# The norms of a decoder layer: nine events placed in a list, a smaller held part, and the embedding's product inside the norm

## The chip, the cores and the metric

One core of a Trainium2 chip runs the whole layer in one launch. The metric is device time in microseconds (us), median of the runs shown. The engines are named as in the profile: PE multiplies matrices (PEld is its loading of weights), DVE and ACT are the vector and the scalar engine, POOL does a little, SP issues nearly all transfers (SPq). Each engine executes its own instructions in the order in which the program lists them.

## The reference, cut to what matters

256 tokens of width 2048 pass through a layer with four layer norms. `alpha` is 2 to the power 1/4.

```python
def layer_norm(x, g, b):
    mu = jnp.mean(xf, axis=-1, keepdims=True)
    var = jnp.mean(jnp.square(xf - mu), axis=-1, keepdims=True)
    y = (xf - mu) * lax.rsqrt(var + LN_EPS)
    return (y * g.astype(jnp.float32) + b.astype(jnp.float32)).astype(x.dtype)
...
h = layer_norm(alpha * h + 0.5 * swiglu(h, w_ffn1_gu[i], w_ffn1_down[i]), ln_g[i, 0], ln_b[i, 0])
...
mixed = (jax.nn.sigmoid(gate_r) * ret_branch + jax.nn.sigmoid(gate_a) * att_branch) @ w_mix_out[i]
h = layer_norm(alpha * h + mixed, ln_g[i, 1], ln_b[i, 1])
h = layer_norm(alpha * h + 0.5 * swiglu(h, w_ffn2_gu[i], w_ffn2_down[i]), ln_g[i, 2], ln_b[i, 2])
ple = jax.nn.sigmoid(h @ w_ple_gate[i]) * (p[i] @ w_ple_proj[i])
h = layer_norm(alpha * h + ple, ln_g[i, 3], ln_b[i, 3])
```

The first three norms are the ones that the change touches. They are called here the first norm (after the first feed-forward part, tiles f1y), the second (after the mixers, mixy) and the third (after the second feed-forward part, f2y). `p @ w_ple_proj` depends on no norm; the kernel computes it early and puts it by.

## The kernel before, in words

**Products and chunks.** Every float32 product is made of three: each operand is split into a high and a low part, and `Sum.add` (L291 to L293) issues low x high, high x high, high x low, each 128x128 by 128x512. Weights come in chunks of 512 KB. A chunk is loaded by SP (L105) into one slot, and then made (`split`, L91 and L92): ACT casts it into a slot of high parts, DVE subtracts into a slot of low parts, and the raw slot is free again. The 256 tokens are two tiles, t = 0 and t = 1. One chunk serves two depths kk of 128, so it is 2 x 3 matmuls for each t, 12 for both.

**Slots.** All chunks and most other tiles live in 46 slots of 4 KB per partition. `fill` (L184 on) lists loads and makes ahead of the products: `room["slots"]` is the number of slots that chunks may take, `room["ahead"]` how much work of PE shall be made beforehand (a plain chunk counts 12), `room["far"]` the same for loads; no make is listed while `room["quiet"]` is set. A slot is taken again only after its last reader is done.

**A norm.** It must not stop PE, so it is spread over both token tiles. `held_out` (from L399) runs the last chunks of the product before the norm ("held" chunks) for t = 0 only, keeps them, then runs them for t = 1. These are called the first and the second pass. After the first pass `Norm.normal(0)` is listed: DVE adds the last columns (`columns`), takes the statistics, computes 1/sqrt in nine small steps (`rsqrt`) and normalises the first 512 columns in two halves (L478, L479). Within the second pass, `turn(0, c)` for c = 0 to 3 normalises 512 further columns on DVE (`more`, one group ahead, listed before the rest of the turn), lets PE transpose group c (`ln_turn`, L486, four transposes), ACT cast and DVE subtract it into the next product's left operand (`ht`, L91 and L92). `run` is given the counts at which the four turns stand: a count is three matmuls (one kk of one chunk, t = 1). After the second pass `normal(1)` is listed.

Then the next product starts in `Norm.first`: six chunks for t = 0, kept, then the same six for t = 1; `turn(1, c)` stands at given counts of chunks. `quiet` is set in the last two steps of the first pass and taken back at the last turn of `first`.

**What differs between the three.** The first norm holds 3 pairs x 2 columns = 6 chunks (f1_down) and `first` belongs to the first block of the mixers (w_rv). The second holds 5 chunks of w_mix (`HELD_MIX`), and `first` belongs to the first block of the second feed-forward part. The third holds 6 chunks (f2_down), and `first` belongs to the gate of the embedding (w_pg). After the first and the second norm's second pass, `put_by` computes two blocks of `p @ w_ple_proj` (four matmul groups of six, tiles pp), copies them by ACT and stores them; it stands between the second pass and `first`.

Of the kernel before, what the change touches and what calls it, by code (L numbers as in the profile page):

```python
# [15 lines left out]
P = 128  # L16
# [10 lines left out]
KF = FF // P  # L27


HELD_MIX = 5  # L30
FRONT = 6
FRONT_PAIRS = 3
HELD_PAIRS = 3
SLOTS = 46


# [12 lines left out]
def layer(ctx: ExitStack, tc: tile.TileContext, io):  # L49
# [163 lines left out]
    def done(u):  # L213
        room["used"] -= u.keeps
        fill()
# [4 lines left out]
    def quiet(on):  # L220
        room["quiet"] = on
# [272 lines left out]
    class Norm:  # L494
# [32 lines left out]
            else:  # L527
                ln_turn(*args, 4 * c, 4, self.keep.get(c))

        def run(self, steps, lhs, turns):  # L530


            self.vectors = vectors.pop()
            self.new = big.tile([P, KD, 512], F32R, tag="ht", name=f"ht{self.i}")
            per = len(steps) // len(self.cols)

            def of_columns(t, j):
                if (j + 1) % per == 0 and j + 1 < len(steps):
                    self.columns(t, j // per)

            def between(n):
                for c, when in enumerate(turns):
                    if n == when:
                        self.turn(0, c)

            held_out(steps, lhs, self.sums, of_columns, lambda: self.normal(0), between)
            self.normal(1)

        def put_away(self):
            if self.away is not None:  # L550
                for c in range(4):
                    sync.dma_start(self.away[c], self.y[c])

        def first(self, steps, lhs, sums, turns):

            def hook(n):
                for c, when in enumerate(turns):
                    if n == when:  # L560
                        self.turn(1, c)

            kept = []
            for j, (key, k0, n) in enumerate(steps):
                u = take(key)
                kept.append(u)
                tokens_chunk(u.chunk, k0, lhs, [sums[t][n] for t in range(2)], (0,))
                fill()
                hook(j + 1)
                if j + 1 == max(turns):  # L570
                    quiet(False)
            for j, (key, k0, n) in enumerate(steps):
                tokens_chunk(kept[j].chunk, k0, lhs, [sums[t][n] for t in range(2)], (1,))
                done(kept[j])
                hook(len(steps) + j + 1)
                if len(steps) + j + 1 == max(turns):
                    quiet(False)
            quiet(False)
            self.put_away()

    def block_stats(stats, y, col):
# [21 lines left out]
            split(pt[:, :, :S], pt[:, :, S:], raw)  # L603
            p_parts.append(pt)

    def put_by(blks):

        pt = p_parts.pop()
        lhs = lambda k: (pt[:, k, :S], pt[:, k, S:])
        done_blks = []  # L610
        for blk in blks:
            u = take(("w_pp", blk, 0))
            ps = banks(f"pp{blk}")
            tokens_chunk(u.chunk, 0, lhs, [Sum(b, 2) for b in ps], (0, 1))
            done(u)
            done_blks.append((blk, ps))
        for blk, ps in done_blks:
            v = slot([P, 2, 512], F32, f"pps{blk}")
            for t in range(2):
                act.copy(v[:, t], ps[t])  # L620
            pp[blk] = dram.tile([P, 2, 512], F32, name=f"ppd{blk}")
            sync.dma_start(pp[blk], v)
# [69 lines left out]
    def gu_keys(name, j):  # L692
        return lambda n, p: (name + "_gu", j, n, p)

    def down_units():
# [11 lines left out]
        return first, second + [("P", p) for p in rest[:-HELD_PAIRS]], rest[-HELD_PAIRS:]  # L707

    def down_keys(name, b):
        return lambda n, p: (name + "_down", 2 * b + n, p)  # L710
# [1 line left out]
    def plan_ffn(name):  # L712
        for j in range(KF // 4):
            block_units(gu_units(j), gu_keys(name, j))
        first, second, held = down_units()
        block_units(first, down_keys(name, 0))
        block_units(second, down_keys(name, 1))
        plan.extend(Single(down_keys(name, 1)(n, p)) for n in range(2) for p in held)

    def ffn(name, i, ht, norm, keep, residual, keepers, away):  # L720
# [28 lines left out]
        for j in range(KF // 4):  # L749
            pg, pu = banks(f"{name}g{j}"), banks(f"{name}u{j}")  # L750
            units = gu_units(j)
            plain = len(units) - sum(kind == "S" for kind, p in units)
            n_of = {(0, 0): KD, (0, 1): KD, (1, 0): KD, (1, 1): KD}
            for kind, p in units:
                if kind == "S":
                    for at in ((0, 0), (0, 1), (1, 0)):
                        n_of[at] -= 1
                    n_of[1, 1] -= 2
            sums = [[Sum((pg, pu)[n][t], n_of[t, n]) for n in range(2)] for t in range(2)]
            got = []  # L760

            if norm is not None and j == 0:
                front, units = units[:FRONT_PAIRS], units[FRONT_PAIRS:]
                steps = [(gu_keys(name, 0)(n, p), 2 * p, n) for _, p in front for n in range(2)]
                norm.first(steps, rhs, sums, (2, 3, 4, 6))
                slots_for_weights(24)

            def before(u, j=j, offset=KD // 2 - len(units)):
                u += offset
                if j == 0 and norm is None and u % 2 == 0:  # L770
                    first_chunk(u // 2)
                    if u == 6:
# [12 lines left out]
            if got:  # L785
                g, v = got
                for x, ps in ((g, pg), (v, pu)):
                    for t in range(2):
                        dve.tensor_tensor(x[:, t], x[:, t], ps[t], ALU.add)  # L789
                act.activation(g, g, AF.Silu)  # L790
                dve.tensor_tensor(v, g, v, ALU.mult)
            else:
                v = slot([P, 2, 512], F32, f"{name}v{j}")
                for t in range(2):
                    act.activation(v[:, t], pg[t], AF.Silu)
                for t in range(2):
                    dve.tensor_tensor(v[:, t], v[:, t], pu[t], ALU.mult)
            later(2, lambda j=j, v=v: turned(j, v))
# [10 lines left out]
        first, second, held = down_units()  # L809
        n_of = {}  # L810
        for b, units in enumerate((first, second + [("P", p) for p in held])):
            s = sum(kind == "S" for kind, p in units)
# [28 lines left out]
            block_stats(stats, y, n)  # L841


        last_ahead = 160 if i < 2 else 136
        last = {}
        for at, (kind, p) in enumerate(second + [("P", p) for p in held]):
            last[p // 2] = at
# [10 lines left out]
        pt_ = [banks(f"{name}e{t}") for t in range(2)]  # L858
        sums = [[Sum(pt_[t][n], n_of[1][t, n]) for n in range(2)] for t in range(2)]
        block(f"{name}d1", second, down_keys(name, 1), lhs, forms, sums, fold(1), before_unit)  # L860
        slots_for_weights(30, last_ahead, last_ahead + 24)
        steps = [(down_keys(name, 1)(n, p), 2 * p, n) for n in range(2) for p in held]

        def combine(sl, p):
            dve.tensor_tensor(sl, sl, p, ALU.add)

        norm = Norm((2, 3), sums, combine, y, stats, i, 4 * LN_EPS, keepers, away)
        norm.run(steps, lhs, (8, 9, 11, 12))
        return norm


# [45 lines left out]
    def mixers(ht, norm, residual, keepers, away):  # L917
# [17 lines left out]

        ps = banks("rv0")
        sums = [[Sum(ps[t], KD)] for t in range(2)]
        norm.first([(("w_rv", 0, c), 2 * c, 0) for c in range(FRONT)], rhs, sums, (2, 3, 4, 6))
        slots_for_weights(24)
        for c in range(FRONT, KD // 2):  # L940
            u = take(("w_rv", 0, c))
# [287 lines left out]
        sums = [[Sum(ps[t], KD)] for t in range(2)]  # L1229
        make_for_norm()  # L1230
        first = KD // 2 - HELD_MIX
        slots_for_weights(28, 148, 172)
        for c in range(first):
            u = take(("w_mix", 3, c))
            tokens_chunk(u.chunk, 2 * c, lhs, [sums[t][0] for t in range(2)], (0, 1))
# [1 line left out]
            run_side()  # L1237
        steps = [(("w_mix", 3, c), 2 * c, 0) for c in range(first, KD // 2)]
        norm = Norm((3,), sums, combine, y, stats, 1, LN_EPS, keepers, away)
        norm.run(steps, lhs, (8, 9, 10, 10))  # L1240
        return norm


    def embedding(ht, norm, y):
# [17 lines left out]
        for blk in range(4):  # L1262
# [4 lines left out]
            if blk == 0:  # L1267
                for j in range(4):
                    pp[j] = load_columns(pp, j, "ppr")
                steps = [(key + (c,), 2 * c, 0) for c in range(FRONT)]  # L1270
                norm.first(steps, lhs, [[s] for s in sums], (4, 5, 6, 8))
                slots_for_weights(24)
                for c in range(FRONT, KD // 2):
                    u = take(key + (c,))
# [53 lines left out]
    with tc.manual_schedule():  # L1328
# [118 lines left out]
```

## Time and profile before

| | us |
|---|---|
| median of 3 runs (2318.96 to 2320.65) | 2319.98 |
| profiled execution | 2320.46 |
| its span, first to last instruction | 2318.6 |
| PE busy in the span | 2281.9 (98%) |
| DVE busy | 1871.6 (81%) |
| ACT busy | 1163.8 (50%) |
| idle time of PE ahead of the transposes of the three norms | 9.9, 3.1 and 2.6 |

The time of the execution is 1.9 us more than the span. A row of the timeline gives the start, the duration, the engine, the line, the operation, the tiles (written <- read) and in brackets the idle time ahead of it with what ended it. The view by windows gives for each stretch the busy time of each engine with its count of instructions, then the granted TensorE clock (1.00 is full), the busy share of the transfer engines and GB/s.

### The profile page before, as it was taken

The numbers are of one execution on the slowest core, as the hardware profiler recorded it, in microseconds if no ns is written. First come the engines' busy times: TensorE is split into PE (matmuls) and PEld (weight loads), VectorE is DVE, ScalarE is ACT, GpSimd is POOL, SyncE is SP. The second block draws the span as 40 slices with busy tenths as digits, with TensorE's granted clock in tenths as the row PEclk, the third lists the DMA queues.
The fourth block names the chain that finished last, engine by engine and source line by source line (L and its number), as shares of the span: only waits on it lengthen the run. The fifth ranks groups of instructions, "written<-read, shape, count | busy, mean of one in ns | idle before, by whom it ended". The sixth has DMA issues, their size and how long they took to land.

```text
span 2318.6 us, 28626 instructions
## 1 busy us (share of the span) xinstructions
PE 2281.9 (98%) x10502; PEld 1889.0 (81%) x10502; DVE 1871.6 (81%) x2348; ACT 1163.8 (50%) x1404; POOL 96.9 (4%) x53
## 2 busy tenths in 40 slices
PE   9999999999998999999999999999999999999997
PEld 7788888888886888888777888788888888888876
DVE  7999999988987774677555555779999999889876
ACT  5565555565553342434544534345555565555532
POOL 0000000000000430133000000000000000000000
PEclk9999999999998999999999999999999999999999
DMA  9566666665585565546556657476666566565771
GB/s 315 164 217 192 195 209 195 193 215 190 197 290 225 193 216 166 172 146 200 156 162 182 190 187 274 161 253 188 196 198 205 179 199 218 190 217 191 273 271 55
DMA packets 193724, 465.69 MB, mean 201 GB/s; under 512 B 14768, under 2 KB 16048, under 8 KB 193584
## 3 DMA queue, kind: packets, MB, share of 16 engines
q1 hardware_dynamic: 191456, 460.91, 60.4%
q10 hardware_dynamic: 2128, 2.97, 0.4%
q8 instruction: 82, 1.34, 0.2%
q14 instruction: 58, 0.48, 0.1%
HBM read 455.43 MB, written 8.39 MB: 200 GB/s over the span
## 4 chain that ended last, share of the span: by engine, by line
PE 94%; DVE 4%; DMA 1%; issue 1%; ACT 0%; SPq 0%; DVEq 0%; ACTq 0%
PE f2g L291 3%; PE f2g L293 3%; PE f2g L292 3%; PE gt L291 3%; PE f1g L291 3%; PE f1g L292 3%; PE f1g L293 3%; PE rqk L242 3%; PE gt L292 3%; PE gt L293 3%; PE f2u L291 2%; PE f2u L292 2%; PE f2u L293 2%; PE f1u L291 2%; PE f1u L292 2%; PE f1u L293 2%
## 5 line engine op out<-in xcount | busy, mean ns | idle before, releaser
L92 DVE TENSOR_TENSOR lf_gu<-rf_gu,hf_gu 128x1024 fp32r<-128x1024 f32 (+1 forms) x283 | 334.5, 1215 | 10.5 <-ACT hf_gu L91 10.1
L91 ACT CAST hf_gu<-rf_gu 128x1024 fp32r<-128x1024 f32 (+1 forms) x283 | 282.1, 1046 | 22.3 <-DMA rf_gu<-in_f_gu 21.4
L92 DVE TENSOR_TENSOR lw_in_f<-rw_in_f,hw_in_f 128x1024 fp32r<-128x1024 f32 x148 | 208.1, 1439 | 61.7 <-ACT hw_in_f L91 59.1
L92 DVE TENSOR_TENSOR lf_down<-rf_down,hf_down 128x1024 fp32r<-128x1024 f32 x152 | 181.1, 1220 | 29.8 <-ACT hf_down L91 24.7
L91 ACT CAST hf_down<-rf_down 128x1024 fp32r<-128x1024 f32 x152 | 155.6, 1051 | 80.3 <-DMA rf_down<-in_f_down 26.4
L91 ACT CAST huf_gu<-uf_gu 128x1024 fp32r<-128x1024 f32 x70 | 73.8, 1054 | 159.2 <-DVE uf_gu L164 153.4
L91 ACT CAST hw_in_f<-rw_in_f 128x1024 fp32r<-128x1024 f32 x148 | 145.9, 1052 | 0.2
L291 PE MATMUL gt<-hw_in_f,ht 128*128 128x512 f32 x256 | 102.5, 400 | 0.0
L291 PE MATMUL f1g<-hf_gu,xt 128*128 128x512 f32 x247 | 97.2, 394 | 5.3 <-ACT hf_gu L91 5.3
L292 PE MATMUL gt<-hw_in_f,ht 128*128 128x512 f32 x256 | 99.9, 390 | 0.0
L293 PE MATMUL gt<-lw_in_f,ht 128*128 128x512 f32 x256 | 99.9, 390 | 0.0
L293 PE MATMUL f1g<-lf_gu,xt 128*128 128x512 f32 x247 | 97.1, 393 | 0.0
L292 PE MATMUL f1g<-hf_gu,xt 128*128 128x512 f32 x247 | 97.0, 393 | 0.0
L291 PE MATMUL f2g<-hf_gu,ht 128*128 128x512 f32 x247 | 96.4, 390 | 0.0
L293 PE MATMUL f2g<-lf_gu,ht 128*128 128x512 f32 x247 | 96.2, 389 | 0.0
L292 PE MATMUL f2g<-hf_gu,ht 128*128 128x512 f32 x247 | 96.1, 389 | 0.0
L91 ACT CAST hvf_gu<-vf_gu 128x1024 fp32r<-128x1024 f32 x70 | 73.8, 1054 | 29.2 <-DVE vf_gu L166 29.1
L92 DVE TENSOR_TENSOR luf_gu<-uf_gu,huf_gu 128x1024 fp32r<-128x1024 f32 x70 | 85.3, 1218 | 0.0
L92 DVE TENSOR_TENSOR lvf_gu<-vf_gu,hvf_gu 128x1024 fp32r<-128x1024 f32 x70 | 85.3, 1218 | 0.0
L790 ACT ACTIVATE eve<-eve 128x1024 f32<-128x1024 f32 x20 | 21.2, 1062 | 126.7 <-DVE eve L789 126.7
L291 PE MATMUL f1u<-hf_gu,xt 128*128 128x512 f32 x212 | 83.6, 394 | 0.0
L291 PE MATMUL f2u<-hf_gu,ht 128*128 128x512 f32 x212 | 83.5, 394 | 0.0
(1053 smaller groups left out, 6278.8 us busy)
## 6 DMA issues: line engine op xcount, KB each, us to landing
rf_gu<-in_f_gu SPq DMA_DIRECT2D x351, 512.0 KB, 4.9
rf_down<-in_f_down SPq DMA_DIRECT2D x176, 512.0 KB, 4.5
rw_in_f<-in_w_in_f SPq DMA_DIRECT2D x148, 512.0 KB, 3.9
rw_rv<-in_w_rv SPq DMA_DIRECT2D x32, 512.0 KB, 4.6
rw_ret<-in_w_ret SPq DMA_DIRECT2D x32, 512.0 KB, 4.3
rw_mix<-in_w_mix SPq DMA_DIRECT2D x32, 512.0 KB, 4.7
rw_pg<-in_w_pg SPq DMA_DIRECT2D x32, 512.0 KB, 5.4
rw_att<-in_w_att SPq DMA_DIRECT2D x16, 512.0 KB, 3.9
```

Of the source, the lines that this page charges most:

```text
L91: act.copy(dst_hi, src)
L92: (lo_engine or dve).tensor_tensor(dst_lo, src, dst_hi, ALU.subtract)
L242: pe.matmul(ps[f], hi[:, kk, f * P : (f + 1) * P], rhs(k), start=k == 0, stop=k == n_k - 1,)
L291: pe.matmul(o, al, bh, start=first, stop=False)
L292: pe.matmul(o, ah, bh, start=False, stop=False)
L293: pe.matmul(o, ah, bl, start=False, stop=self.left == 0)
L790: act.activation(g, g, AF.Silu)
```

## The change

1. `run` and `first` no longer hold fixed hooks. A norm has nine events in one order: `turn(0, 0)` to `turn(0, 3)`, `normal(1)`, `turn(1, 0)` to `turn(1, 3)`; `follow` fires the next ones when a count is reached. The lists given to `run` and `first` say at which counts.
2. For the first and the second norm, `put_by` runs inside `run`, right after the second pass, and the turns of t = 0 stand among its four groups of six matmuls. Its product is now ordered by t within a chunk.
3. `HELD_MIX` is 4 (was 5); the first norm holds 2 pairs = 4 chunks (was 6), the third still 3 pairs.
4. The first and second norm want 136 ahead (160 and 148 before), the third as before; the slots for chunks while the norm runs are 27, 26 and 27 (30, 28 and 30 before).
5. `quiet` ends at the ninth event instead of the last hook of `first`.

```diff
-HELD_MIX = 5
+HELD_MIX = 4
...
-HELD_PAIRS = 3
+HELD_PAIRS = 2, 3
...
+        def follow(self, n, times):
+            while times and times[0] == n:
+                times.pop(0)
+                at, self.at = self.at, self.at + 1
+                if at == 4:
+                    self.normal(1)
+                else:
+                    self.turn(at // 5, at % 5)
+                if at == 8:
+                    quiet(False)
+
-        def run(self, steps, lhs, turns):
+        def run(self, steps, lhs, times, blks=()):
...
+            self.at, times = 0, list(times)
...
-            def between(n):
-                for c, when in enumerate(turns):
-                    if n == when:
-                        self.turn(0, c)
-
-            held_out(steps, lhs, self.sums, of_columns, lambda: self.normal(0), between)
-            self.normal(1)
+            held_out(steps, lhs, self.sums, of_columns, lambda: self.normal(0), lambda n: self.follow(n, times))
+            if blks:
+                put_by(blks, lambda n: self.follow(2 * len(steps) + n, times))
+            assert not times
...
-    def put_by(blks):
+    def put_by(blks, between):
...
-            tokens_chunk(u.chunk, 0, lhs, [Sum(b, 2) for b in ps], (0, 1))
-            done(u)
+            sums = [Sum(b, 2) for b in ps]
+            for t in range(2):
+                tokens_chunk(u.chunk, 0, lhs, sums, (t,))
+                if t:
+                    done(u)
+                between(2 * j + t + 1)
...
-                norm.first(steps, rhs, sums, (2, 3, 4, 6))
+                norm.first(steps, rhs, sums, (4, 6, 7, 8))
...
-        last_ahead = 160 if i < 2 else 136
+        last_ahead = 136
...
-        slots_for_weights(30, last_ahead, last_ahead + 24)
+        slots_for_weights(27, last_ahead, last_ahead + 24)
...
-        norm.run(steps, lhs, (8, 9, 11, 12))
+        norm.run(steps, lhs, *(((8, 10, 11, 12, 12), (0, 1)) if i < 2 else ((8, 11),)))
...
-        norm.first([(("w_rv", 0, c), 2 * c, 0) for c in range(FRONT)], rhs, sums, (2, 3, 4, 6))
+        norm.first([(("w_rv", 0, c), 2 * c, 0) for c in range(FRONT)], rhs, sums, (4, 6, 7, 8))
...
-        slots_for_weights(28, 148, 172)
+        slots_for_weights(26, 136, 160)
...
-        norm.run(steps, lhs, (8, 9, 10, 10))
+        norm.run(steps, lhs, (8, 10, 11, 12, 12), (2, 3))
...
-                norm.first(steps, lhs, [[s] for s in sums], (4, 5, 6, 8))
+                norm.first(steps, lhs, [[s] for s in sums], (1, 3, 3, 6, 7, 9, 10))
...
         norm = ffn("f1", 0, ht, None, x_parts, x_columns, (), rows[0])
-        put_by((0, 1))
         norm = mixers(norm.new, norm, rows[0], kept, rows[1])
-        put_by((2, 3))
         norm = ffn("f2", 2, norm.new, norm, norm.keep, rows[1], (), None)
```

In `first` the two hooks are replaced by `self.follow(j + 1, times)` and `self.follow(len(steps) + j + 1, times)`, with the same products around them. A list of `run` counts three matmuls each through the second pass and then six matmuls each through `put_by`: with four held chunks the second pass ends at 8, and 9 to 12 are the groups of `put_by`. A list of `first` counts chunks: 1 to 6 for t = 0, 7 to 12 for t = 1. So the first two norms have `turn(0, 0)` at the end of the second pass, the other three of t = 0 and `normal(1)` in `put_by`, and the turns of t = 1 at 4, 6, 7 and 8 chunks of `first`. The third norm has two turns in the second pass (counts 8 and 11), the other two and `normal(1)` after 1, 3 and 3 chunks of `first`, and the turns of t = 1 after 6, 7, 9 and 10.

More of the change, by code (lines that the diff above doesn't have):

```diff
@@ L552, in put_away, with first @@
                     sync.dma_start(self.away[c], self.y[c])
[L554 to L563, printed above, removed]
+        def first(self, steps, lhs, sums, times):
+            kept, times = [], list(times)
             for j, (key, k0, n) in enumerate(steps):
@@ L568, in first @@
                 fill()
-                hook(j + 1)
-                if j + 1 == max(turns):
-                    quiet(False)
+                self.follow(j + 1, times)
             for j, (key, k0, n) in enumerate(steps):
@@ L574, in first @@
                 done(kept[j])
[L575 to L578, printed above, removed]
+                self.follow(len(steps) + j + 1, times)
+            assert self.at == 9
             self.put_away()
@@ L610, in put_by @@
         done_blks = []
-        for blk in blks:
+        for j, blk in enumerate(blks):
             u = take(("w_pp", blk, 0))
             ps = banks(f"pp{blk}")
-            tokens_chunk(u.chunk, 0, lhs, [Sum(b, 2) for b in ps], (0, 1))
-            done(u)
+            sums = [Sum(b, 2) for b in ps]
[4 more added lines that the diff above has]
+                between(2 * j + t + 1)
             done_blks.append((blk, ps))
@@ L693, in gu_keys, with down_units @@
         return lambda n, p: (name + "_gu", j, n, p)
-    def down_units():
+    def down_units(n_held):
         first = []
@@ L706, in down_units @@
                 second += [("S", 2 * g + e), ("P", rest.pop(0))]
-        return first, second + [("P", p) for p in rest[:-HELD_PAIRS]], rest[-HELD_PAIRS:]
+        return first, second + [("P", p) for p in rest[:-n_held]], rest[-n_held:]
     def down_keys(name, b):
@@ L714, in plan_ffn @@
             block_units(gu_units(j), gu_keys(name, j))
-        first, second, held = down_units()
+        first, second, held = down_units(HELD_PAIRS[name == "f2"])
         block_units(first, down_keys(name, 0))
@@ L808, in ffn @@
         made = {}
-        first, second, held = down_units()
+        first, second, held = down_units(HELD_PAIRS[name == "f2"])
         n_of = {}
```

## The prediction

> **What bounds the kernel now.** I read the engines' shares first, then the waits of PE, then the timeline around the three norms, then the clock by windows. Rows of the page and of the waits (waited in all, times, longest):
>
> ```profile
> PE 2281.9 (98%) x10502; PEld 1889.0 (81%) x10502; DVE 1871.6 (81%) x2348; ACT 1163.8 (50%) x1404; POOL 96.9 (4%) x53
> ...
> PE lnps L486 <- DVE f1y L479: 9.9, 3, 8.9
> ...
> PE lnps L486 <- DVE mixy L479: 3.1, 5, 1.4
> PE lnps L486 <- DVE f2y L479: 2.6, 4, 1.6
> ```
>
> PE sets the end, and the change takes no matmul away. It can only move the 15.6 us in which PE waits ahead of the transposes (L486), and what these waits cost in clock. First norm, timeline, the transfers by windows and SP's waits:
>
> ```profile
> 699.97 4.43 SPq L105 DMA_DIRECT2D rw_rv<-in_w_rv  x4
> ...
> 703.61 1.05 ACT L91 CAST hw_rv<-rw_rv 128x1024 fp32r<-128x1024 f32 x1 [7.33 <-PE f1e L291]
> ...
> 704.69 2.48 DVE L92 TENSOR_TENSOR lw_rv<-rw_rv,hw_rv 128x1024 fp32r<-128x1024 f32 x2 [3.66 <-ACT hw_rv L91]
> ...
> 707.09 0.68 DVE L865 TENSOR_TENSOR f1y<-f1y,f1e 128x512 f32<-128x512 f32 x1
> ...
> 712.95 0.66 PE L486 MATMUL lnps<-ident,f1y 128*128 128x128 f32 x2 [8.93 <-DVE f1y L479]
> ...
> 696.00:700.00 4.00, 4.00 (x19) 3.30 (x18) 3.95 (x5) 0.28 (x1) 0.00 (x0) 1.00 0.00 0
> ...
> SPq L105 <- PE f1e L293: 15.6, 3, 10.9
> ```
>
> The reader should see a chain. PE starts the second pass at 698.4 (24 matmuls, 0.227 us start to start, ahead of the transposes). DVE could begin the norm then, but its list has two makes of w_rv ahead of it. Their loads left only at 699.97: from 696 to 700 nothing was moved, SP waited 10.9 us for a slot that PE frees in the second pass. So the norm began at 707.09, 8.7 us late.
>
> Clock, the column behind POOL, in windows of 4 us:
>
> ```profile
> 709.00:713.00 4.00, 0.05 (x1) 0.08 (x2) 3.62 (x14) 0.00 (x0) 0.00 (x0) 0.50 0.33 132
> ...
> 717.00:721.00 4.00, 4.00 (x15) 3.31 (x14) 3.57 (x6) 0.59 (x1) 0.00 (x0) 0.50 0.00 0
> ...
> 1500.00:1504.00 4.00, 1.93 (x11) 1.21 (x11) 3.93 (x8) 1.79 (x3) 0.00 (x0) 1.00 0.36 139
> ...
> 2208.00:2212.00 4.00, 3.07 (x10) 2.56 (x11) 3.93 (x8) 0.59 (x1) 0.00 (x0) 0.65 1.02 409
> ```
>
> After a wait PE may run at half clock: after 8.93 us, and after the 1.62 us of the third norm, but not in the second, with 2.07 us idle of 4.
>
> What each norm costs now, from the start of the second pass to the end of the last transposes: 698.42 to 737.49, 1491.84 to 1520.37, 2200.14 to 2228.02, that is 39.1, 28.5, 27.9. Their work: 96, 90 and 84 matmuls of 0.227 and eight groups of transposes of 0.45 (0.36 and a slower first matmul): 25.4, 24.0, 22.6. **Excess: 13.7, 4.5 and 5.3 us.**
>
> **The change, part by part.**
>
> *Fewer chunks wanted at the first norm.* By the rules of `fill`, before: 14 chunks are held or ready (6 + 2 w_pp + 6 w_rv), with the load and the make of the last two w_rv listed back to back after the last plain chunks. After: 12 (4 + 2 + 6), with one load listed ahead of each make. The third norm of before is the nearest row: 12 chunks, its last load issued at 2193.3, 6.8 us ahead of the second pass, its last make done at 2199.56. The first norm after needs three slots more (trig, pt, praw) and two less (the activations of p = 11 are done earlier); 24 + 13 leave some nine of 46. So I take the makes as done when the first pass ends. Cost bounds: nothing, or again the 8.7 us (rivals).
>
> *Turns of t = 0 in put_by.* DVE's chain, rows of the third norm from its last columns (2200.80): first half normalised +4.4, second +5.3, `columns` of t = 1 +6.6, then `more` 1, 2, 3 done +8.1, +10.2, +12.2 (2208.88, 2210.99, 2213.03). It starts 0.2 after the first pass. PE comes to the turns at 5.4 (eight counts of 0.68), 8.6, 10.4 and 12.3 us (groups of 1.36, 0.45 per turn). Waits: 0.1, 0, 0.1, 0.2.
>
> *normal(1).* It is now listed behind turn(0, 3) and covered by four chunks of `first`, 5.44 us; before, `put_by` and two chunks, 8.2 us, covered it with no wait. The row of the third norm gives its length: transposes at 2213.54, the halves done at 2219.79 and 2220.71 (+6.3, +7.2). PE, back from the transposes after 0.45, comes at 5.9: it waits 0.4, and after two transposes about 0.8. Later turns: 0.1. Excess of the first norm after: 0.4 + 1.3 and 0.3 for slower matmuls behind transposes, 2.0. **Gain 11.7** (bounds 9 and 13).
>
> *Second norm.* Same lists. Before, DVE made chunks until 1493.17, 1.2 us past the first pass; with four held, the first pass ends 1.36 us later in the same stream of chunks, so DVE is just free. Only one column, so the `more` come 1.4 us earlier; the copies to `keep` (0.4 to 0.6 on ACT) lie beside PE. Excess after: 0.3 + 1.3 + 0.3 = 1.9. **Gain 2.6** (bounds 1 and 4).
>
> *Third norm.* Nothing of its chunks changes ahead of the norm. turn(0, 1) goes from count 9 to 11, so its wait falls from 1.62 to 0.4. But only three chunks lie between turn(0, 3) and turn(1, 0), and turn(1, 0) stands right ahead of the first chunk of t = 1, which reads its result. DVE's rows there, before:
>
> ```profile
> 2213.54 0.60 PE L486 MATMUL lnps<-ident,f2y 128*128 128x128 f32 x4
> ...
> 2219.31 0.48 DVE L479 SCALAR_TENSOR_TENSOR f2y<-f2y,rstd,ln_b 128x256 f32<-128x256 f32 x1
> 2219.71 0.48 DVE L478 SCALAR_TENSOR_TENSOR f2y<-f2y,mv,ln_g 128x256 f32<-128x256 f32 x1
> 2220.23 0.48 DVE L479 SCALAR_TENSOR_TENSOR f2y<-f2y,rstd,ln_b 128x256 f32<-128x256 f32 x1
> 2220.63 0.74 DVE L478 SCALAR_TENSOR_TENSOR f2y<-f2y,mv,ln_g 128x512 f32<-128x512 f32 x1
> 2221.41 0.75 DVE L479 SCALAR_TENSOR_TENSOR f2y<-f2y,rstd,ln_b 128x512 f32<-128x512 f32 x1
> 2222.08 0.75 DVE L92 TENSOR_TENSOR ht<-lnps,ht 128x256 fp32r<-128x256 f32 x2
> ```
>
> The low part of the transposed halves (L92) is queued behind `more` (1.4 us); its first half is done 1.8 after the second normalised half. From the start of the second pass: turn(0, 3) at 14.45; the halves at 20.7 and 21.6; PE comes at 14.45 + 0.45 + 3 x 1.36 = 19.0, waits 1.8, then 0.7, then, from 22.1, until the low part at 23.4, 1.3: 3.8 us idle of 4.5. With 0.2 + 0.4 ahead, 0.2 behind and 0.3 of slower matmuls: 4.9. A wait of 1.62 us took the clock here before; the slow matmuls and transposes behind it cost 6 x 0.2 + 0.6 = 1.8. I take 1.5, as some of the slow stretch falls into waits; bounds 0 (second norm) and 3.6 (first norm, 8.1 us at half). Excess 6.4 against 5.3: **loss 1.1** (bounds: gain 0.4, loss 3.2).
>
> [...]
>
> *Later end of quiet, smaller allowance in the third norm, reordered put_by.* Taken at nothing. The makes of the chunks after `first` now start with four chunks (5.4 us) left instead of six, in the third norm with two (2.7); the cast (1.05) and the low part (1.2) of one chunk and the last turn (1.3) lie beside them. In the third norm that is just enough; without that cover it costs 1 us. SP only has w_pg loads behind. put_by issues the same 24 matmuls, four copies and two stores, now behind turn(0, 3) on ACT, needed only by the embedding.
>
> **Sum:** 11.7 + 2.6 - 1.1 = 13.2. The profiled execution took 2320.46, 1.9 outside its span of 2318.6, which I leave alone: 2307.3. It stands 0.5 above the median, so against 2319.98 I say **2306.8**.
>
> **The rivals.**
>
> *The clock stays at full in the third norm*, as in the second with half the window idle; against it stand 3.8 idle of 4.5 us and the 0.65. [...]
>
> *The last load of the first two norms hangs on the last plain chunk.* Its slot is free 5.44 us ahead of the end of the first pass; issue 0.35, landing 4.39 (the row of w_rv before), cast 1.05, low part 1.22 make 7.0, so the norm starts 1.5 late, twice: 2309.8. For it: one spare load is all that 27 and 26 leave over 24. Against: spare slots of the 46.
>
> *The first norm's loads still hang on the first held chunk*, as in the row at 699.97. Then its excess stays and 1.5 us of the gain remain: 2318.5, no change that can be told. For it: in that row SP waited though my count leaves slots free, so the count is not the whole of it. Against: the third norm with 12 chunks has no such wait.
>
> *Slower: that wait in the first and the second norm.* 26 slots for 24 wanted leave the second norm no load ahead, so its last f_gu load could leave only when a held chunk is done. Its excess would go from 4.5 to the 13.7 of the first norm: 0 - 9.2 - 1.1, 2330.3. It decides from a start about 5 us late in both. Against: with 28 the loads needed left by 1485.23, 6.6 ahead of the second pass.
>
> **How the numbers follow.** Forecast 0.50, clock at full 0.20, late last load 0.13, first norm unchanged 0.10, both norms late 0.07. The range 2302.5 to 2312.5 holds the first three, 0.83: its low end is all upper bounds (13 + 4 + 0.4), its high end 9 + 1.5 - 3. What can be told from no change is about 0.2%, 4.6 us: faster is 0.50 + 0.20 + 0.13 = 0.83, same 0.10, slower 0.07.
>
> **What would show it.** Right: no wait above 1 us ahead of the first norm's first transposes, both last w_rv makes of DVE ahead of its first `columns`, loads running in the 4 us ahead of the second pass; waits of some 0.4 and 0.8 us at turn(1, 0) of the first two norms; in the third, PE idle 3 to 4 us around turn(1, 0), part of it at the first w_pg matmul of t = 1 waiting for DVE L92, and a clock below 1.00 behind. Wrong: a wait of several us at the first transposes, an ACT cast of w_rv or f_gu waiting for a late load, or a PE that idles at the first chunk after `first`.

## The result, and the profile after

The changed kernel takes 2313.86 us (median of 11 runs, 2311.94 to 2316.42), the kernel before, beside it, 2320.65 (11 runs, 2318.96 to 2322.07). The ratio is 0.9972 with an interval of 0.9963 to 0.9982: faster, by 6.8 us (0.3%), about half of the 13.2 forecast, and outside the range. The profiled execution took 2312.8 with a span of 2311.0. Its matmuls are as many as before and its PE is 99% busy.

The waits of PE after (waited in all, times, longest):

```profile
PE lnps L486 <- DVE f1y L479: 3.5, 3, 2.8
PE lnps L486 <- DVE f2y L479: 2.8, 4, 1.6
PE pg L291 <- DVE ht L92: 1.3, 1, 1.3
PE lnps L486 <- DVE mixy L479: 1.2, 3, 0.5
```

The first norm's 9.9 us have become 3.5, and 0.5 more put down to ACT, where 1.7 were forecast; the second's 3.1 are 1.2; the third has as much as before and a new wait at the first chunk of t = 1. The timeline after around the first norm, with SP, ACT, DVE and PE put together in order of time:

```profile
695.41 0.80 SPq L105 DMA_DIRECT2D rw_rv<-in_w_rv  x2
...
699.03 1.05 ACT L91 CAST hw_rv<-rw_rv 128x1024 fp32r<-128x1024 f32 x1 [1.11 <-DMA rw_rv<-in_w_rv]
700.11 1.23 DVE L92 TENSOR_TENSOR lw_rv<-rw_rv,hw_rv 128x1024 fp32r<-128x1024 f32 x1 [0.81 <-ACT hw_rv L91]
700.34 1.05 ACT L91 CAST hw_rv<-rw_rv 128x1024 fp32r<-128x1024 f32 x1 [0.27 <-DMA rw_rv<-in_w_rv]
702.27 1.23 DVE L92 TENSOR_TENSOR lw_rv<-rw_rv,hw_rv 128x1024 fp32r<-128x1024 f32 x1 [0.94 <-PE f1e L292]
703.42 0.68 DVE L870 TENSOR_TENSOR f1y<-f1y,f1e 128x512 f32<-128x512 f32 x1
...
709.27 0.41 PE L486 MATMUL lnps<-ident,f1y 128*128 128x128 f32 x2 [2.78 <-DVE f1y L479]
...
724.57 0.41 PE L486 MATMUL lnps<-ident,f1y 128*128 128x128 f32 x2 [0.35 <-DVE f1y L479]
725.49 0.41 PE L486 MATMUL lnps<-ident,f1y 128*128 128x128 f32 x2 [0.51 <-ACT ht L91]
```

The second pass starts at 700.89. The last two loads of w_rv wanted ahead of the norm leave together at 695.41 and 695.83, when PE has finished the last plain chunk (5.44 us ahead of the second pass). Their casts run at 699.03 and 700.34, and the last low part starts only at 702.27: its row waits for PE f1e L292, a reader of the first held chunk, and PE is done with that chunk 1.36 us into the second pass. So the norm's columns start at 703.42, some 2.3 us late, and PE waits 2.78 us at the first transposes. The waits of turn(1, 0), 0.35 and 0.51, are near those of the forecast (0.4 and 0.8).

The windows after, with the granted clock behind POOL:

```profile
709.00:713.00 4.00, 3.31 (x10) 2.62 (x11) 3.90 (x8) 0.74 (x2) 0.00 (x0) 0.59 0.16 66
...
2208.00:2212.00 4.00, 2.32 (x11) 1.43 (x9) 3.61 (x14) 0.04 (x1) 0.00 (x0) 1.00 0.29 117
2215.00:2219.00 4.00, 4.00 (x14) 3.23 (x13) 1.89 (x4) 0.59 (x1) 0.00 (x0) 0.58 0.79 224
```

The clock falls behind the first norm's wait and behind the third's three waits. These are, in the timeline of PE:

```profile
2211.49 0.44 PE L486 MATMUL lnps<-ident,f2y 128*128 128x128 f32 x2 [1.60 <-DVE f2y L479]
2212.49 0.41 PE L486 MATMUL lnps<-ident,f2y 128*128 128x128 f32 x2 [0.57 <-DVE f2y L479]
2214.18 0.50 PE L291 MATMUL pg<-hw_pg,ht 128*128 128x512 f32 x1 [1.28 <-DVE ht L92]
```

The excess of a norm (as in the prediction: from the start of the second pass to the end of the last transposes, less 0.227 us for a matmul and 3.6 for the transposes) went from 13.7, 4.5 and 5.3 to **6.3, 2.4 and 7.0**. That is 7.4 + 2.1 - 1.7 = 7.8, against a difference of the spans of 7.6 (2318.6 to 2311.0), so the rest of the kernel takes about as long as before.

### The profile page after: what moved, and what is told of

Same layout as the page of the kernel before. It is cut to its first block, busy times and chain, and to the rows that moved or that the text cites. A ratio compares the mean times of both kernels' runs of the same rounds, so it can differ in the third digit from the quotient of the medians.

```text
span 2311.0 us, 28634 instructions
## 1 busy us (share of the span) xinstructions
PE 2279.6 (99%) x10502; PEld 1887.7 (82%) x10502; DVE 1871.4 (81%) x2348; ACT 1162.9 (50%) x1404; POOL 97.0 (4%) x53
## 4 chain that ended last, share of the span: by engine, by line
PE 95%; DVE 3%; issue 1%; DMA 0%; ACT 0%; DVEq 0%; ACTq 0%
PE f2g L293 3%; PE f2g L291 3%; PE f2g L292 3%; PE f1g L291 3%; PE gt L291 3%; PE f1g L292 3%; PE f1g L293 3%; PE rqk L242 3%; PE gt L292 3%; PE gt L293 3%; PE f2u L291 2%; PE f2u L292 2%; PE f2u L293 2%; PE f1u L292 2%; PE f1u L291 2%; PE f1u L293 2%
## 5 line engine op out<-in xcount | busy, mean ns | idle before, releaser
L292 PE MATMUL gt<-hw_in_f,ht 128*128 128x512 f32 x256 | 99.9, 390 | 0.0
L292 PE MATMUL f1g<-hf_gu,xt 128*128 128x512 f32 x247 | 96.9, 392 | 0.0
L292 PE MATMUL f2g<-hf_gu,ht 128*128 128x512 f32 x247 | 96.1, 389 | 0.0
```

Of the source, the lines that this page charges most:

```text
L292: pe.matmul(o, ah, bh, start=False, stop=False)
```

## The experiments

All are edits of the changed kernel. The two theories on the first norm are called in the texts below the slots theory (its last loads and makes wait for slots that PE gives back late) and the supply theory (more is wanted too late). The medians, each with that of the kernel before run beside it, and the readings and the excess in the profiled execution:

| kernel | first wait of the first norm | excess of the three norms | median, us | before, beside it | ratio to before (95%) |
|---|---|---|---|---|---|
| before | 8.93 | 13.7, 4.5, 5.3 | 2320.65 | | |
| changed | 2.78 | 6.3, 2.4, 7.0 | 2313.86 | 2320.65 | 0.9963 to 0.9982 |
| praw split early | 4.03 | 7.7, 2.4, 7.3 | 2313.47 | 2319.91 | 0.9956 to 0.9980 |
| amount raised earlier | 2.79 | 5.3, 2.4, 6.4 | 2311.83 | 2319.91 | 0.9951 to 0.9976 |
| 14 chunks wanted | 8.85 | 12.2, 2.4, 7.2 | 2320.10 | 2319.91 | 0.9992 to 1.0009 |
| third norm as before | 4.09 | 8.3, 2.4, 4.5 | 2313.16 | 2319.91 | 0.9955 to 0.9980 |
| eleven chunks | 1.03 | 3.6, 2.4, 7.0 | 2310.53 | 2320.21 | 0.9946 to 0.9971 |
| third: order swapped | 2.79 | 6.0, 2.4, 5.4 | 2312.10 | 2320.21 | 0.9950 to 0.9977 |
| third: other places | 4.66 | 8.5, 2.4, 3.5 | 2310.45 | 2320.21 | 0.9944 to 0.9971 |
| third: swap and places | 4.08 | 7.3, 2.4, 3.3 | 2310.32 | 2320.21 | 0.9941 to 0.9969 |
| eleven, other places | 2.29 | 6.0, 2.4, 4.2 | 2306.59 | 2320.02 | 0.9930 to 0.9955 |
| eleven, swap, places | 0.90 | 3.5, 2.4, 3.8 | 2306.67 | 2320.02 | 0.9933 to 0.9958 |
| ten chunks | 0.30 | 13.2, 2.4, 3.3 | 2317.89 | 2320.02 | 0.9981 to 0.9999 |
| ten, praw split early | under 0.15 | 10.5, 2.4, 3.8 | 2316.20 | 2320.02 | 0.9975 to 0.9994 |

Of the first eight edits only that with 14 chunks has an interval that does not overlap the changed kernel's. For the other seven the times alone decide nothing, and the argument rests on the waits and the excess of one profiled execution each.

### Fewer chunks wanted: undone for the first norm

```diff
-        last_ahead = 136
+        last_ahead = 160 if i == 0 else 136
...
-        slots_for_weights(27, last_ahead, last_ahead + 24)
+        slots_for_weights(30 if i == 0 else 27, last_ahead, last_ahead + 24)
```

> The changed kernel, with the first norm wanting 160 ahead with 30 slots as before the change (14 chunks held or ready instead of 12); held chunks, places of the events and the other two norms as changed. If the fewer chunks wanted are what brought the first norm's gain (slots theory): the loads of w_rv chunks 6 and 7 leave only in the second pass, the last low part is done some 8 to 9 us after its start, PE waits 8 to 9 us ahead of the first transposes as before the change, and the kernel is at 2320 to 2323. If the new places of the events brought it: the wait stays near 2.8 us and the time near 2313.9.

Measured: 2320.10 us, no change against the kernel before. Its waits of PE:

```profile
PE lnps L486 <- DVE f1y L479: 9.4, 3, 8.9
```

The loads of chunks 6 and 7 left at 702.97 and behind it, 1.55 us into the second pass, and the columns came at 710.02. So in the first norm wanting two chunks fewer is worth some 5 to 6 us of excess (12.2 against 6.3 in the changed kernel's profile, and 7.3 in the middle of five profiles, see below), and holding fewer chunks with the new places about 1.5 (13.7 to 12.2).

### More wanted earlier

```diff
-                45 if u < len(second) - 5 else last_ahead
+                45 if u < len(second) - (7 if i == 0 else 5) else last_ahead
```

> The changed kernel, with the amount wanted ahead of the first norm raised two units sooner (from unit 13 of the second f1_down block instead of 15). Supply theory: the loads of w_rv leave earlier, the norm starts on time, PE's first wait of the first norm falls from 2.8 us to under 1 and the kernel to about 2310.5. Slots theory: the loads of w_rv chunks 4 and 5 still leave with the end of the last plain chunk and the last low part still waits for the first held chunk, so the wait stays within 0.5 us of 2.8 and the time near 2313.9.

Measured: the first wait is 2.79. The windows of this run:

```profile
692.00:696.00 4.00, 4.00 (x19) 3.30 (x18) 4.00 (x5) 1.88 (x2) 0.00 (x0) 1.00 0.00 0
709.00:713.00 4.00, 3.32 (x16) 2.65 (x17) 3.89 (x8) 0.74 (x2) 0.00 (x0) 1.00 0.32 131
```

The early loads did leave earlier, and then the queue stood still: nothing is moved from 692 to 696, where the changed kernel moved 235 GB/s. The last two loads left from 695.63 on, again with the last plain chunk, and the last low part began at 702.26, again behind PE. The supply theory falls. The median lies 8.1 us under that of the kernel before beside it, the changed kernel's 6.8. This run's excess is 1.6 lower. At the first norm it is 1.0 lower with the same waits: the clock of the second row stayed at 1.00 behind the wait that took it to 0.59 there. The other 0.6 are at the third norm, whose list is the same. Whether the edit does any of that, or chance, is open.

### The slots handed on one place earlier

```diff
-            if u == len(second) - 1:
+            if u == (15 if i == 0 else len(second) - 1):
                 make_for_norm()
```

> The changed kernel, with the split of the embedding's input (praw to pt) listed at unit 15 of the second f1_down block instead of at its last unit. Nothing else differs; in the list of who takes whose slot, each w_rv chunk from the third on moves up by one place, so the low part of w_rv chunk 5 no longer takes the slot of the first held chunk. Slots theory (the first norm starts 2.5 us late because the last loads and makes of w_rv wait for slots): the last low part starts 0.9 us earlier, PE's first wait of the first norm falls from 2.8 to about 1.9 us, the kernel from 2313.9 to about 2313.0; the rest of the lateness (1.5 us, the loads that leave only with the last plain chunk) stays. Supply theory (more is wanted too late, so that loads and makes start too late): nothing moves, 2.8 us and 2313.9.

Measured: the first wait grew to 4.03. The timeline of DVE in this run:

```profile
702.04 2.46 DVE L92 TENSOR_TENSOR lw_rv<-rw_rv,hw_rv 128x1024 fp32r<-128x1024 f32 x2 [2.66 <-ACT hw_rv L91]
```

The number expected is missed: the two loads that leave at the last plain chunk's end landed 2 us later than in the changed kernel's profile, and the columns started at 704.42. The last low part does not wait for PE here, as the slots theory says, but this run can't show that the edit does it. With loads so late, the held chunk is given back before the low part's turn comes. The next run has the changed kernel's own list ahead of the first norm, and late loads too, and its low parts wait for PE as little:

```profile
702.23 2.55 DVE L92 TENSOR_TENSOR lw_rv<-rw_rv,hw_rv 128x1024 fp32r<-128x1024 f32 x2 [2.14 <-ACT hw_rv L91]
```

### The third norm at its old places

```diff
-        norm.run(steps, lhs, *(((8, 10, 11, 12, 12), (0, 1)) if i < 2 else ((8, 11),)))
+        norm.run(steps, lhs, *(((8, 10, 11, 12, 12), (0, 1)) if i < 2 else ((8, 9, 11, 12, 12),)))
...
-                norm.first(steps, lhs, [[s] for s in sums], (1, 3, 3, 6, 7, 9, 10))
+                norm.first(steps, lhs, [[s] for s in sums], (4, 5, 6, 8))
```

> The changed kernel, with the events of the third norm at the places of the kernel before: turns of t = 0 at counts 8, 9, 11, 12, normal(1) at 12, turns of t = 1 at chunks 4, 5, 6, 8 of the product that follows. If the new places cost the third norm 1.7 us (excess 7.0 against 5.3, three chunks only between the last turn of t = 0 and the first of t = 1): the three waits around the first turn of t = 1 (1.6, 0.6, 1.3) go, the wait of 1.6 us at the second turn of t = 0 comes back, and the kernel is at about 2312.2. If they cost nothing and the difference is the clock of that one execution: 2313.9.

Measured: the excess of the third norm is 4.5 against 7.0, of the three waits only the 0.57 is left in full (0.26 instead of 1.60, none at the first chunk of t = 1), 1.63 at the second turn is back, and the clock stayed full (no w_pg matmul from 2208 to 2220 takes more than 0.48 us). The kernel before had a clock of 0.65 behind its wait of 1.62 there, so a part of the 2.5 may be chance. In time nothing is seen: the median is 6.8 us under that of the kernel before beside it, as the changed kernel's is. So the loss at the new places stands in the waits, not in the medians. In the profile the first norm, of which not a line differs, took 8.3 instead of 6.3. Here are the rows of the transfers between 694 and 703, count, size and median time from issue to landing, of the changed kernel and then of this run:

```profile
rw_rv<-in_w_rv SPq DMA_DIRECT2D x3, 512.0 KB, 3.6
```

```profile
rw_rv<-in_w_rv SPq DMA_DIRECT2D x3, 512.0 KB, 5.7
```

The same loads, issued at 695.4 in both, land 2 us later in one execution than in the other. Five profiles have the same list ahead of the first norm (the changed kernel and the four that differ in the third norm alone): first waits 2.78, 4.09, 2.79, 4.66, 4.08 and excess 6.3, 8.3, 6.0, 8.5, 7.3. In the first, the second and the fourth of these the load that leaves first at the last plain chunk's end lands after 3.6, 5.7 and 6.3 us. The changed kernel's profile is thus a good one; with the middle value, 7.3, the sum is 6.4 + 2.1 - 1.7 = 6.8, which is the difference of the medians. So close a match is partly luck, since each excess comes from one execution.

### One chunk fewer at the first norm

```diff
-        last_ahead = 136
+        last_ahead = 124 if i == 0 else 136
...
-        norm.first([(("w_rv", 0, c), 2 * c, 0) for c in range(FRONT)], rhs, sums, (4, 6, 7, 8))
+        norm.first([(("w_rv", 0, c), 2 * c, 0) for c in range(FRONT - 1)], rhs, sums, (4, 6, 7, 8))
```

> The changed kernel, with one chunk fewer wanted at the first norm: 124 ahead instead of 136, and the product that follows begins with five held chunks of w_rv instead of six, so that the sixth is made behind the norm. Slots theory: the first norm starts late because the last two w_rv loads leave only when the last plain chunk gives its slots back, 5.4 us ahead of the second pass, and land 3.6 to 5.7 us later (two executions of the same list: 3.6 and 5.7); with five chunks one of these two drops out of the way together with its cast and its low part (2.3 us). The first wait of the first norm falls from 2.8 to 4.1 us (seen so far) to 0.2 to 2 us, and the kernel to 2310 to 2312; up to 1 us may come back as a wait at the sixth chunk. If the makes of DVE ahead of the norm are not what the norm waits for: 2.8 or more, 2313.9.

Measured: 2310.53, first wait 1.03, excess 3.6, clock full (1.00 from 708 to 712). The last low part ahead of the norm starts at 700.88, before the first held chunk is given back, and does not wait for PE. No wait came back at the sixth chunk. One load that the norm waits for still leaves with the last plain chunk, and how it lands decides: the same list had a first wait of 2.29 in another run below, 0.90 in a third.

### Ten chunks, and ten with the slots one place earlier

```diff
-        last_ahead = 136
+        last_ahead = 112 if i == 0 else 136
...
-                if at == 8:
+                if at == (6 if self.i == 0 else 8):
                     quiet(False)
...
-        norm.first([(("w_rv", 0, c), 2 * c, 0) for c in range(FRONT)], rhs, sums, (4, 6, 7, 8))
+        norm.first([(("w_rv", 0, c), 2 * c, 0) for c in range(FRONT - 2)], rhs, sums, (4, 6, 7, 8))
```

Both have the third norm of the run "other places" below; the second of the two also has the early split of praw shown above.

> As the run with eleven chunks and new places, but with ten chunks at the first norm (four held w_rv chunks, 112 ahead), and quiet taken back at the second turn of t = 1 of the first norm. DVE has one chunk less to make; but the load of the last made w_rv chunk again takes a slot of the last plain chunk (its activations), so that it leaves 5.4 us ahead of the second pass as the last one of eleven does. Slots theory: the first wait of the first norm stays at 0.3 to 2 us, as with eleven. If it is the amount of making on DVE or of loading: 0.2 to 0.3 us. A wait of about 1 us is expected at the last turns of t = 1, where DVE now makes chunks. Time 2306 to 2309.

> As the run with ten chunks, with the split of the embedding's input listed at unit 15 instead of the last: the same chunks and the same makes, but the slots are passed on one place earlier, and the load of the last made w_rv chunk takes a slot of the plain chunk ahead of the last one, given back 2.7 us sooner. Slots theory: that load leaves 8 us ahead of the second pass, all makes are done when the norm begins, and the first wait is 0.2 to 0.4 us however the load lands. If the order of slots does not matter: as with ten chunks.

Measured, timeline of SP and ACT, first with ten chunks, then with the early split too (the issue of the last load that is made ahead of the norm, and its cast):

```profile
695.38 0.33 SPq L105 DMA_DIRECT2D rw_rv<-in_w_rv  x1
...
698.89 1.05 ACT L91 CAST hw_rv<-rw_rv 128x1024 fp32r<-128x1024 f32 x1 [3.88 <-DMA rw_rv<-in_w_rv]
```

```profile
691.86 0.33 SPq L105 DMA_DIRECT2D rw_rv<-in_w_rv  x1
...
696.23 1.05 ACT L91 CAST hw_rv<-rw_rv 128x1024 fp32r<-128x1024 f32 x1 [1.86 <-DMA rw_rv<-in_w_rv]
```

With the second pass at 701.08 and 699.83, the load left 5.7 us ahead of it with ten chunks, and 8.0 with the same ten chunks and the slots in another order. That is the slots theory's pair of numbers (5.4 and 8), and neither the amount wanted nor DVE's work differs between the two. The first wait is 0.30 in the one (its load landed quickly) and below 0.15 in the other.

Both miss the time expected (2306 to 2309) by some 9 us, for another reason: a wait of about 1 us had been thought of. With four chunks in `first`, turn(1, 0) stands right ahead of the first chunk of t = 1, which waits 1.28 us for its low part; a later chunk waits 1.40 for the low part of turn(1, 1); and the makes let loose at turn(1, 1) stand on DVE ahead of what turn(1, 3) needs. The timeline of DVE, and then PE, with ten chunks:

```profile
730.51 4.63 DVE L92 TENSOR_TENSOR lw_rv<-rw_rv,hw_rv 128x1024 fp32r<-128x1024 f32 x4 [0.26 <-ACT hw_rv L91]
735.06 2.35 DVE L92 TENSOR_TENSOR lw_in_f<-rw_in_f,hw_in_f 128x1024 fp32r<-128x1024 f32 x2
...
738.91 1.12 PE L486 MATMUL lnps<-ident,f1y 128*128 128x128 f32 x4 [5.12 <-DVE f1y L479]
```

Six makes, 7 us of DVE, where one was thought of: once `quiet` is off, `fill` lists as much as the slots allow.

### The third norm: order and places

```diff
         def turn(self, t, c):
             args = self.y, t, self.i, self.new
-            if c < 3:
+            early = t and c == 0 and self.i == 2
+            if c < 3 and not early:
                 self.more(t, c + 1)
...
+            if early:
+                self.more(t, c + 1)
```

> The changed kernel, with one order changed in the third norm: at the first turn of t = 1 the transposes with their cast and low part are listed ahead of the normalising of the next 512 columns, not behind it. If the low part (L92) queued behind that normalising is what PE waits for at the first chunk of t = 1: the wait of 1.28 us there goes, the waits of 1.6 and 0.6 us ahead of the transposes stay, excess of the third norm 7.0 to about 5.7, and the kernel about 1.3 us faster than the changed one, less or more by what the first norm's loads do. If something else ends that wait: it stays at 1.0 to 1.3 us.

Measured: the wait of 1.28 for the low part is gone, 1.58 and 0.57 are still there, and a new one of 0.87 stands at turn(1, 1), whose columns are normalised later now. The excess is 5.4 (expected 5.7), but not in the way expected. The new wait gives back most of the 1.28, so the waits are only 0.4 us less in all; the other 1.2 is the clock: no w_pg matmul from 2208 to 2220 takes more than 0.50 us, where the changed kernel has rows of 0.63. So the nearness to 5.7 is luck in part.

```diff
-        norm.run(steps, lhs, *(((8, 10, 11, 12, 12), (0, 1)) if i < 2 else ((8, 11),)))
+        norm.run(steps, lhs, *(((8, 10, 11, 12, 12), (0, 1)) if i < 2 else ((8, 11, 12),)))
...
-                norm.first(steps, lhs, [[s] for s in sums], (1, 3, 3, 6, 7, 9, 10))
+                norm.first(steps, lhs, [[s] for s in sums], (1, 1, 5, 6, 7, 8))
```

> The changed kernel, with other places for the events of the third norm: turns of t = 0 at counts 8, 11 and 12 of the second pass and after the first chunk of the product that follows, normal(1) there too, turns of t = 1 after 5, 6, 7 and 8 chunks. Four chunks instead of three now lie between the last turn of t = 0 and the first of t = 1, and one chunk of t = 0 between that turn and the first chunk that reads its result. By the durations of the chain: waits of 0.2, 0.4, 1.0 and 0.2 us at the turns of t = 0, 0.2 and 0.7 at the first turn of t = 1, 0.4 at the first chunk of t = 1; excess about 3.3 with the clock at full, against 7.0 (changed) and 4.5 (old places). If the clock falls after the wait of 1.0: 4.5.

Measured: waits of 0.23, 0.76, 0.26 and 0.57, none at the first chunk of t = 1, clock full (no w_pg matmul from 2208 to 2220 above 0.48 us): excess 3.5 as the chain of durations gave (3.3), though single waits are off (1.0 and 0.4 had been expected where 0.76 and none came). The median is 9.8 us under that of the kernel before beside it, 3.0 more than the changed kernel's, although its profile has the latest first norm of those with the changed kernel's list (4.66).

> The changed kernel, with the order of the run before (transposes ahead of the next normalising at the first turn of t = 1) and the third turn of t = 0 after the first chunk, the fourth and normal(1) after the second chunk instead of the third: four chunks between them and the first turn of t = 1, which stays right ahead of the first chunk of t = 1. By the durations of the chain: waits of 0.2 and 0.4 at the turns of t = 0, 0.3 and 0.5 at the first turn of t = 1, 0 to 0.4 at the first chunk of t = 1; no clock drop; excess of the third norm about 2.4. If the time between normal(1) and the first turn is not what decides, its wait stays at 1.6 and the excess at 5 or more.

Its edit is the swap above with `norm.first(..., (1, 2, 2, 6, 7, 9, 10))`. Measured: 0.25 and 0.57 at turn(1, 0) instead of 1.60 and 0.57, nothing at the first chunk of t = 1, 0.85 at turn(1, 1): excess 3.3, 0.9 above the 2.4 expected. Four chunks instead of three between normal(1) and turn(1, 0) are what takes the 1.6 away.

### Both norms

> The changed kernel with two of the changes tried: eleven chunks at the first norm (five held w_rv chunks, 124 ahead) and the third norm's events at counts 8, 11, 12 and after 1, 1, 5, 6, 7, 8 chunks. If the two add up: excess of the three norms 2 to 4.5 (3.65 seen), 2.4 and 3.5 against 6.3, 2.4 and 7.0 of the changed kernel, and a time of 2306 to 2309. If the one undoes the other (the first norm's waits vary with the landing of its loads): 2310.5 as each alone.

> Eleven chunks at the first norm, and in the third norm the transposes of the first turn of t = 1 ahead of the next normalising, with events at counts 8 and 11 and after 1, 2, 2, 6, 8, 9 and 10 chunks: two chunks instead of one between the first and the second turn of t = 1, where 0.85 us of waiting was seen. Excess of the third norm about 2.5, of the first 2 to 4.5; time 2305.5 to 2308.

Measured: 2306.59 and 2306.67, ratios 0.9943 and 0.9946. The two gains add up: 13.4 us under the kernel before, where the changed kernel has 6.8 and the edits alone 2.9 and 3.0 more. Both kernels are faster than the changed one: their intervals do not overlap its interval. The second run missed its third norm (excess 3.8, about 2.5 expected): moving turn(1, 1) one chunk on did take away the 0.85, but the low part of that turn then came too late for its own reader:

```profile
2212.97 0.50 PE L291 MATMUL pg<-hw_pg,ht 128*128 128x512 f32 x1 [1.40 <-DVE ht L92]
```

## Why the prediction was half right

**The step that failed** is the one that sized the first norm: "So I take the makes as done when the first pass ends", from a count that "leaves some nine of 46" slots. The count was right and did not decide. What the traces show is that the last two loads leave only at the end of the last plain chunk, 5.44 us ahead of the second pass, and that the last low part waits 0.94 us for PE's last reader of the first held chunk; and, in the runs with ten chunks, that the same chunks with the slots handed on in another order let the last load leave 8.0 instead of 5.7 us ahead. The reason is read from the built program, and no trace shows it: each tile gets the slot that was given back longest ago in the order that the builder assumes, and that is fixed. When the last low part of w_rv takes its slot, ten slots of tiles already used up are free (seven raw tiles of made chunks, praw and the two tiles of the fold), but they stand in line behind those of the held chunks. SP's wait in the profile before pointed to it (the third rival says that "the count is not the whole of it"). The nearest row taken, the third norm with 12 chunks, did not carry over; no run tests what differs there.

The first norm's excess was put at 2.0 and is 6.3 in the profiled execution, 7.3 in the middle of five: a gain of 7.4 or 6.4 instead of 11.7. In the terms of its sum, the waits at the turns of t = 0 were put at 0.4 us and measured 3.2 (2.78 and 0.42), those at the turns of t = 1 were put at 1.3 and measured 0.9, and the slowed clock, 1.2 us of matmuls, was put at nothing (the 0.3 in the sum is for matmuls behind transposes). The first norm alone is 4.3 to 5.3 us of the 6.4 that are missing; the rest is the second and the third norm, 0.5 and 0.6 short. The range's high end, "9 + 1.5 - 3", does not use the bounds given with the parts, which are 9, 1 and a loss of 3.2; these would give 2313.2. The measured time lies outside that as well, because the first norm's gain fell below its bound of 9.

**The second rival had the mechanism**, "the last load hangs on the last plain chunk", for the first norm alone. It put the delay at 1.5 us. Measured were 2.3 in the changed kernel's profile and up to 4.2 in the others, since two loads leave together, not one, since the first of them lands after 3.6 to 6.3 us in three profiles of the same list, and since the low part waits for a held chunk where the loads land early. It was not foreseen that this wait would also take the clock (0.59, 1.2 us of slowed matmuls). The second norm shows nothing of it: DVE's makes end at 1485.49, and the second pass starts at 1485.50.

**Right:** PE's bound and where the time could come from; the second norm (2.1 gained, 2.6 forecast; waits 0.33, 0.31, 0.51 and 0.37); turn(1, 0) of the first norm; and that fewer chunks wanted would bring most of the first norm's gain, shown by undoing it (5 to 6 us of 6.4 to 7.4). The third norm went as worked out, step by step: waits of 1.60, 0.57 and 1.28 us against 1.8, 0.7 and 1.3, the last for the low part queued behind `more` (shown by the swap), the clock down to 0.58 behind them, and a loss of 1.7 against 1.1. The first rival, the clock at full there, is refuted: in all five profiles with this list of the third norm (the changed kernel, the two that moved loads or slots, 14 and eleven chunks) matmuls of 0.63 us instead of 0.39 follow these waits.

**Taken at nothing, and right here:** the later end of `quiet` cost no wait in the profile after. The runs with ten chunks, where it ends two turns sooner, show what makes listed ahead of the last turns cost: 5.12 us at one turn.

## What to carry to other kernels

A free buffer need not be a buffer at hand: where slots are handed on in a fixed order, ask for each load which earlier tile's last reader it follows, and when that reader runs, rather than how many are free. A load that leaves with the end of one known piece of work lands at a time that scatters (here 3.6 to 6.3 us after its issue), so it needs that much room ahead of its use and not the mean. And a turn placed right ahead of its own reader pays for all that is queued before its last step; one piece of other work between them, or that step moved up in the queue, took that wait away here (1.28 us), though 0.87 of it came back at the next turn in the swap.

## What the runs showed of the hardware

- One load of 512 KB, issued at the same place by the same list, took 3.6 us to land in one execution, 5.7 in another and 6.3 in a third. It is not that load alone: the four loads of w_rv issued just before it took 3.4 to 3.9 us in the first execution and 4.2 to 4.4 in the second. The runs do not show why, and whether this makes the spread of the changed kernel's times (2311.9 to 2316.4) is not shown either.
- The same wait of PE, 2.78 and 2.79 us at 709.27 and 709.26, left the clock at 0.59 over the next 4 us in one execution and at 1.00 in another. In a third, with the third norm's order swapped, matmuls of 0.63 us follow a wait of 2.79, as in the first; in the second no matmul of `put_by` takes more than 0.48. The runs do not show why.
